# Four dense steps between the first two score blocks, a second buffer for a head's values, and later flips of the last normalised rows

## The chip, the cores and the metric

The kernel runs on one core of one Trainium2 chip. The metric is the device time of one execution in microseconds (us); the time of a kernel is the median of its runs. A core has a matrix engine (PE, TensorE), a vector engine (DVE), an activation engine (ACT), a general engine (POOL, GpSimd) and a queue engine that mostly issues DMAs (SP). Each works through its own instructions in order, and semaphores make one wait for another. PE reads its operands from on-chip memory (SBUF) and writes to an accumulation memory (PSUM), out of which DVE and ACT take the results. PE runs at 1.2 or 2.4 GHz; the profile gives the granted clock as a share of the full speed.

## The reference, cut to what matters

One layer of a streaming encoder is computed for a prompt of 1024 frames and for 8 decode streams of 16 frames. One input projection feeds two groups of heads: four heads of differential softmax attention and four heads of retention. Then come the output projection and a gated MLP with a causal convolution.

```python
h = rmsnorm(x, g_mix) * (1.0 + sc_m) + sh_m
qa, ka, va, qr, kr, vr, gr = split_projection(h, w_in, pos)
oa = attend(qa, ka, va)
orr, ret_state = retain(qr, kr, vr)
oa = rmsnorm(oa, g_sub_a) * (1.0 - lam_init)
...
def diff_attention_block(q, k, v, q_pos, k_pos, rel_bias, lam):
    ...
    def probs(qi, ki):
        s = jnp.einsum('bqhd,bkhd->bhqk', qi, ki).astype(jnp.float32) * scale + bias
        return jax.nn.softmax(jnp.where(visible, s, NEG_INF), axis=-1)
    p = (probs(q[..., :A_QK_DIM], k[..., :A_QK_DIM])
         - lam * probs(q[..., A_QK_DIM:], k[..., A_QK_DIM:]))
    return jnp.einsum('bhqk,bkhd->bqhd', p.astype(v.dtype), v)
```

For the prompt there are 8 query blocks of 128 rows in each of 4 heads. Block qb sees (qb + 1) * 128 keys, so the work of a block grows from 128 to 1024 columns. Each block needs two softmaxes, one for each half of the query and key vectors.

## The kernel before

The span falls into stages: norms and the conditioning vectors with the first projections (to about 238 us), prompt attention (238 to 460), decode attention (460 to 560), retention (560 to 650), output projection, up-projection and down-projection. The change touches the prompt attention alone.

**Two kinds of work on PE.** The attention loop (L695) runs over n_ = 8 * head + block. For each block it computes the scores of the next block (`scores`, L617: matmuls at L626 into two PSUM tiles `sc`, one for each softmax), flips the weights of the current block with PE transposes (`flip`, L649), and multiplies the flipped weights with the values (`weighted`, L661). Between these three, `fill(ns)` puts in dense steps. A dense step is one pass of the input projection for another head or another stage, three matmuls (L62, L63, L64) on the same accumulator `dn`. In the text a D is one such step. The numbers in `f_scores`, `f_flip` and `f_out` say for how many nanoseconds, by the program's own account, dense steps are put in; a 384-column D counts 480, a 256-column one 320. A step is taken only as long as the unit of work it belongs to lies below the limit `prog["lim"]`. The units are, in order, the k and q projections of heads 0 to 3 (two units for each head, 24 D's of 384 columns each), then 256-column units for retention. While head 0 runs, the limit is 4, so the stock is the 48 D's of head 1's k and q.

**What one block asks of the other engines.** After the scores, DVE adds the bias (L629), takes the row maximum (L631), and ACT takes the exponential into `e` and sums it (L632), once for each softmax. DVE then makes the reciprocal (L634), the factor (L635) and the difference of the two softmaxes, `e` in L637. Only then can PE flip `e` (F, L649); ACT copies the flipped tiles out of PSUM (`pT`, L651), and PE multiplies (W, L661). DVE scales the result (L662). The two `sc` tiles exist once for a block's two halves (bufs=2), so scores of the next block need the exponentials of this block to be done.

**Normalised rows.** After blocks 3 and 7 of a head, `small_norm` (L264 to L268, with L131 on DVE and L132 on POOL) normalises four blocks' rows, and `later(5000, ...)` queues `heads_out`: four transposes (H, L670), an ACT copy (L672) and a DMA to `d_m` (L673). A queued function runs in the first `step` or `fill` in which the program's own count of nanoseconds has passed its due time.

**Values and weights.** `load_v` (L611) loads a head's values, 512 KB, into `vt`; before, there is one buffer, so the load of the next head's values waits for the last W of this head. Weights come as `raw` tiles of 256 KB by DMA (L142), are cast by ACT (L58), and the remainder is taken by DVE (L59). Inside the attention loop, PE's order is the order in which the program is written; DVE, ACT, POOL and SP are put in order by a scheduler that works from its own estimates.

**Decode and retention.** After the loop, decode loads `qbd` (L718), `kc` (L728) and others on SP, behind the last `d_m` store, flips the cached keys (L744, copied by ACT at L746 and by DVE) and runs its scores. The 256-column D's left over are used there and in retention, where t = 8 multiplies with the decode streams' states (L1018), updates them (L1025 and L1028), stores them, and loads the next ones (L1047); the prompt blocks follow (L983, L985, L994).

Of the kernel before, what the change touches and what calls it, by code (L numbers as in the profile page):

```python
# [7 lines left out]
F32 = mybir.dt.float32  # L8
# [40 lines left out]
def body(ctx: ExitStack, tc: tile.TileContext, i):  # L49
# [4 lines left out]
    def pool(name, bufs=1, **kw):  # L54
        return tc.tile_pool(name=name, bufs=bufs, **kw)
# [65 lines left out]
    def tp():  # L121
        return psd.tile([128, 4, 128], F32, tag="tp", bufs=2, name="tp")
# [55 lines left out]
    units, pend, prog = [], [], {"cur": None, "bal": 0.0, "now": 0.0, "done": 0, "lim": 99, "rope": None}  # L178
# [4 lines left out]
    def can():  # L183
        return units and prog["done"] + (prog["cur"] is not None) < prog["lim"]
# [5 lines left out]
    def later(ns, fn):  # L190
        pend.append((prog["now"] + ns, fn))
# [17 lines left out]
    def fill(ns):  # L209
        prog["bal"] += ns  # L210
        while prog["bal"] > 0 and (can() or prog["cur"]):
            step()
        if prog["bal"] > 0:
            prog["now"] += prog["bal"]
            prog["bal"] = 0.0
        while pend and pend[0][0] <= prog["now"]:
            pend.pop(0)[1]()
# [317 lines left out]
    with ExitStack() as st:  # L535
        ap = st.enter_context(pool("attn"))
# [3 lines left out]
        def sc():  # L540
            return pva.tile([128, 1024], F32, tag="sc", bufs=2, name="sc")
# [67 lines left out]
            units.append([lambda: load_wt(base, h * 128), lambda w_: dense_t(nm, h, w_), None])  # L609

        def load_v(h):  # L611
            vt = ap.tile([128, 8, 128], F32, tag="vt", bufs=1, name="vt")
            nc.sync.dma_start(vt, i["v_prompt"][:, h * 128:h * 128 + 128].rearrange("(t p) d -> p t d", p=128))
            return vt

        def scores(h, kq, qb):
            khi, klo, qs = (kq[z_] for z_ in ("khi", "klo", "qs"))  # L617
            nk = (qb + 1) * 128
            e = ap.tile([128, 2, SEQ], F32, tag="e", bufs=2, name="e")
            sm = ap.tile([128, 8], F32, tag="sm", bufs=3, name="sm")  # L620
            for hf in range(2):
                s_ = sc()
                for c in range(0, nk, 512):
                    n = min(512, nk - c)
                    for p, kk in enumerate((khi, klo)):
                        T.matmul(s_[:, c:c + n], lhsT=qs[:, hf, qb * 128:qb * 128 + 128],  # L626
                                 rhs=kk[:, hf, c:c + n], start=(p == 0), stop=(p == 1))
                lo_ = max(nk - 256, 0)
                V.tensor_tensor(out=s_[:, lo_:nk], in0=s_[:, lo_:nk],  # L629
                                in1=nb[:, h, 256 - (nk - lo_):256], op=ALU.add)  # L630
                V.tensor_reduce(out=sm[:, hf:hf + 1], in_=s_[:, 0:nk], op=ALU.max, axis=AX.X, negate=True)  # L631
                S.activation(out=e[:, hf, 0:nk], in_=s_[:, 0:nk], func=ACTF.Exp,  # L632
                             bias=sm[:, hf:hf + 1], scale=1.0, accum_out=sm[:, 2 + hf:3 + hf])
            V.reciprocal(out=sm[:, 4:6], in_=sm[:, 2:4])  # L634
            V.scalar_tensor_tensor(out=sm[:, 6:7], in0=sm[:, 2:3], scalar=sm[:, 5:6], in1=nlam,  # L635
                                   op0=ALU.mult, op1=ALU.mult)
            V.scalar_tensor_tensor(out=e[:, 0, 0:nk], in0=e[:, 1, 0:nk], scalar=sm[:, 6:7],  # L637
                                   in1=e[:, 0, 0:nk], op0=ALU.mult, op1=ALU.add)
            return e, sm
# [15 lines left out]
        def weighted(h, vt, qb, e, sm, pTs):  # L655
            if qb % 4 == 0:
                o4s[0] = ap.tile([128, 4, 128], F32, tag="o4", bufs=2, name="o4")
            o4 = o4s[0]
            po = tp()[:, 0]
            for n in range(qb + 1):  # L660
                T.matmul(po[:, 0:128], lhsT=pTs[n // 4][:, n % 4], rhs=vt[:, n], start=(n == 0), stop=(n == qb))  # L661
            V.tensor_scalar_mul(o4[:, qb % 4], po[:, 0:128], sm[:, 4:5])  # L662
            if qb % 4 == 3:
                small_norm(ap, o4, 4)
                later(5000, lambda: heads_out(h, qb, o4))

        def heads_out(h, qb, o4):
            p_ = tp()
            for n in range(4):
                T.transpose(p_[:, n], o4[:, n], ident)  # L670
            om = ap.tile([128, 512], F32, tag="t2", bufs=2, name="om")
            S.activation(out=om, in_=p_.rearrange("p a b -> p (a b)"), func=ACTF.Copy, scale=g_sa)  # L672
            nc.sync.dma_start(d_m[h, :, qb // 4 * 512:qb // 4 * 512 + 512], om)  # L673
# [5 lines left out]
        def spare():  # L679
# [4 lines left out]
        build_nb()  # L684
        drain(2)
        vt = load_v(0)
        cur = (0, vt, 0) + scores(0, kqs[0], 0)
        f_scores = ([1500, 1250, 1150, 1200, 650, 850, 450, 650],
                    [1950, 1850, 1750, 1650, 1550, 1450, 1350, 1250])
        f_flip = ([1925, 1775, 1625, 1475, 1325, 1325, 1475, 1025],  # L690
# [3 lines left out]
        for n_ in range(8 * NH):  # L694
            h, qb = divmod(n_, 8)  # L695
            nxt = None
            if n_ < 8 * NH - 1:
                h2, qb2 = divmod(n_ + 1, 8)
                if qb2 == 0:
                    drain(2 * h2 + 2)  # L700
                    vt = load_v(h2)
# [953 lines left out]
```

## Time and profile before

| what | value |
|---|---|
| time before, median of 3 runs | 1548.28 us (1547.75 to 1548.39) |
| time of the profiled execution | 1546.16 us |
| span of the profiled execution | 1544.3 us |
| PE busy | 1502.5 us, 97% |
| DVE busy | 964.3 us, 62% |
| ACT busy | 601.4 us, 39% |
| POOL busy | 232.2 us, 15% |

The span runs from the first to the last instruction of the profiled execution; 1.86 us of its time lie around the span. Busy time is an average over stages with different limits. The rows that matter are those in which PE waits, since PE is busy almost throughout. In a row of the timeline the first number is the start and the second the duration; matmuls are pipelined, so the time that one costs is the distance between starts, and not its duration.

### The profile page before, as it was taken

To read this page: it belongs to the slowest core of one execution; us is meant where nothing else is said; L and a number is where in the kernel's file an instruction comes from. 1 tells how busy PE (TensorE), PEld (TensorE's weight loads), DVE (VectorE), ACT (ScalarE), POOL (GpSimd) and SP (SyncE) were. 2 spreads that over 40 slices of the span, in tenths; PEclk is the share of its full clock that TensorE was granted. 3 is DMA by queue.
4 is the path that set the end of the run, shared out by engine and by line. 5 is a ranking of instruction groups with operands and counts; after the bars stand their busy time and mean duration, and the time that the engine had idled before them with its cause. 6 is when DMAs were issued, how large, how long until landed. Compare 5 with 4: busy or idle time off the path is not lost.

```text
span 1544.3 us, 27022 instructions
## 1 busy us (share of the span) xinstructions
PE 1502.5 (97%) x10580; PEld 1369.4 (89%) x10580; DVE 964.3 (62%) x1735; ACT 601.4 (39%) x1167; POOL 232.2 (15%) x335
## 2 busy tenths in 40 slices
PE   6999999999999999999999999999999999999998
PEld 5867899999898898878899999999999988888786
DVE  4701237888765424553499877877788758254695
ACT  4501124555332433455564444444444455021212
POOL 1000021111121111343212111110111100000051
PEclk8999999999999999999999999999999999999999
DMA  9865331111319657675532222222222237132232
GB/s 295 270 253 181 121 107 49 54 46 50 110 61 338 217 200 222 224 249 191 171 119 86 82 73 74 72 71 80 77 75 71 80 119 270 35 116 88 95 134 109
DMA packets 191515, 205.98 MB, mean 133 GB/s; under 512 B 11357, under 2 KB 149899, under 8 KB 191388
## 3 DMA queue, kind: packets, MB, share of 16 engines
q1 hardware_dynamic: 172412, 189.31, 37.7%
q10 hardware_dynamic: 18976, 14.95, 3.0%
q8 instruction: 83, 1.36, 0.4%
q14 instruction: 44, 0.36, 0.1%
HBM read 154.66 MB, written 49.56 MB: 132 GB/s over the span
## 4 chain that ended last, share of the span: by engine, by line
PE 56%; DVE 2%; DMA 1%; issue 0%; ACT 0%; SPq 0%; POOL 0%; POOLq 0%; DVEq 0%; ACTq 0%
PE pb L1342 5%; PE pb L1344 5%; PE pb L1343 5%; PE dn L62 3%; PE dn L64 3%; PE dn L63 3%; PE pf L64 3%; PE pf L63 3%; PE pf L62 3%; PE dn L1342 2%; PE dn L1344 2%; PE dn L1343 2%; PE tp L1342 2%; PE tp L1344 2%; PE tp L1343 2%; PE tp L63 2%
## 5 line engine op out<-in xcount | busy, mean ns | idle before, releaser
L62 PE MATMUL dn<-w,hhi 128*128 128x256 f32 x648 | 189.7, 293 | 0.0
L64 PE MATMUL dn<-w,hlo 128*128 128x256 f32 x648 | 181.9, 281 | 0.0
L63 PE MATMUL dn<-w,hhi 128*128 128x256 f32 x648 | 181.6, 280 | 0.0
L62 PEld LDWEIGHTS dn<-w,hhi 128*128 128x128 f32 x648 | 122.5, 189 | 11.4 <-issue 10.2
L64 PEld LDWEIGHTS dn<-w,hlo 128*128 128x128 f32 x648 | 122.6, 189 | 7.5 <-issue 7.5
L63 PEld LDWEIGHTS dn<-w,hhi 128*128 128x128 f32 x648 | 122.7, 189 | 4.3 <-issue 4.2
L1288 DVE SCALAR_TENSOR_TENSOR y<-U,cv,y 128x1168 f32<-128x1168 f32 x88 | 124.2, 1429 | 3.0 <-ACT y L1285 2.1
L58 ACT CAST sl<-raw 128x512 fp32r<-128x512 f32 x65 | 40.3, 622 | 108.8 <-PE pb L1343 93.7
L58 ACT CAST se<-raw 128x512 fp32r<-128x512 f32 x66 | 41.1, 624 | 100.2 <-PE dn L1343 48.4
L62 PE MATMUL dn<-hhi,w 128*128 128x384 f32 x192 | 69.9, 364 | 0.0
L246 POOL TENSOR_TENSOR sg<-sg,rot 128x256 f32<-128x256 f32 x36 | 28.1, 780 | 272.2 <-DVE rot L245 229.5
L63 PE MATMUL dn<-hlo,w 128*128 128x384 f32 x192 | 65.0, 339 | 0.0
L64 PE MATMUL dn<-hhi,w 128*128 128x384 f32 x192 | 65.0, 339 | 0.0
L1294 POOL COPY tails<-U 128x18 f32<-128x18 f32 x44 | 23.7, 538 | 271.7 <-DVE U L1359 183.1
L59 DVE TENSOR_TENSOR w<-raw,w 128x512 fp32r<-128x512 f32 x56 | 39.0, 712 | 37.0 <-ACT w L58 24.7
L1285 ACT ACTIVATE y<-U,cv 128x1168 f32<-128x1168 f32 x44 | 60.2, 1367 | 4.5 <-DVE U L1363 0.5
L1514 DVE TENSOR_TENSOR facc<-facc,pf 128x512 f32<-128x512 f32 x54 | 36.8, 681 | 39.0 <-PE pf L64 39.0
L632 ACT ACTIVATE e<-sc,sm 128x128 f32<-128x128 f32 (+7 forms) x64 | 47.3, 744 | 30.9 <-DVE sm L631 30.1
L62 PE MATMUL dn<-woh,mh 128*128 128x512 f32 x144 | 57.9, 402 | 0.0
L58 ACT CAST w<-raw 128x512 fp32r<-128x512 f32 x56 | 33.3, 619 | 60.3 <-PE dn L63 33.8
L58 ACT CAST ew<-wr 128x512 fp32r<-128x512 f32 x24 | 14.6, 619 | 108.1 <-PE tp L63 84.2
L64 PE MATMUL dn<-woh,ml 128*128 128x512 f32 x144 | 56.5, 393 | 0.0
(427 smaller groups left out, 4861.8 us busy)
## 6 DMA issues: line engine op xcount, KB each, us to landing
wa<-in_w_ada SPq DMA_DIRECT2D x48, 512.0 KB, 8.6
raw<-in_w_up SPq DMA_DIRECT2D x88, 256.0 KB, 2.9
raw<-in_w_in SPq DMA_DIRECT2D x56, 256.0 KB, 4.2
wr<-in_w_down SPq DMA_DIRECT2D x48, 256.0 KB, 3.7
gr<-d_g SPq DMA_DIRECT2D x20, 576.0 KB, 3.7
d_g<-y SPq DMA_DIRECT2D x22, 512.0 KB, 2.6
kc<-in_cache_k SPq DMA_DIRECT2D x8, 1024.0 KB, 7.9
vc<-in_cache_v SPq DMA_DIRECT2D x8, 1024.0 KB
```

What stands on the lines that cost most here:

```text
L58: S.copy(hi, src)
L59: V.tensor_tensor(out=lo, in0=src, in1=hi.bitcast(F32), op=ALU.subtract)
L62: T.matmul(out, lhsT=sh, rhs=mh, start=first, stop=False)
L63: T.matmul(out, lhsT=sh, rhs=ml, start=False, stop=False)
L64: T.matmul(out, lhsT=sl, rhs=mh, start=False, stop=last)
L632: S.activation(out=e[:, hf, 0:nk], in_=s_[:, 0:nk], func=ACTF.Exp, bias=sm[:, hf:hf + 1], scale=1.0, accum_out=sm[:, 2 + hf:3 + hf])
L1285: S.activation(out=y[:, j0:j1], in_=U[:, j0:j1], func=ACTF.Identity, scale=wconv[0][:, kt:kt + 1], bias=bconv[:, kt:kt + 1])
L1288: V.scalar_tensor_tensor(out=y[:, j0:j1], in0=U[:, j0 + j:j1 + j], scalar=wconv[j][:, kt:kt + 1], in1=y[:, j0:j1], op0=ALU.mult, op1=ALU.add)
L1342: T.matmul(o, lhsT=sh, rhs=mh, start=st_, stop=False, skip_group_check=True)
L1343: T.matmul(o, lhsT=sh, rhs=ml, start=False, stop=False, skip_group_check=True)
L1344: T.matmul(o, lhsT=sl_, rhs=mh, start=False, stop=en, skip_group_check=True)
L1514: V.tensor_tensor(out=facc[t][:, sl], in0=facc[t][:, sl], in1=p_, op=ALU.add)
```

## The change

There are three edits, all in the prompt attention. The tile `vt` gets two buffers. `heads_out` of block 7 is queued with 8000 instead of 5000. And behind the scores of the very first block, before the loop, `fill(1920)` with the limit 4 puts in four D's.

```diff
         def load_v(h):
-            vt = ap.tile([128, 8, 128], F32, tag="vt", bufs=1, name="vt")
+            vt = ap.tile([128, 8, 128], F32, tag="vt", bufs=2, name="vt")
...
-                later(5000, lambda: heads_out(h, qb, o4))
+                later(8000 if qb == 7 else 5000, lambda: heads_out(h, qb, o4))
...
         cur = (0, vt, 0) + scores(0, kqs[0], 0)
+        prog["lim"] = 4
+        fill(1920)
```

The number of D's and of every other PE instruction is the same; only their places differ. PE, at the start of the loop, between the scores of block 0 (128 columns) and those of block 1 (256 columns) of head 0:

```order
 L626 MATMUL sc<-khi,qs 128x128
 L626 MATMUL sc<-klo,qs 128x128
+L62 MATMUL dn<-hhi,w 128x384
+L63 MATMUL dn<-hlo,w 128x384
+L64 MATMUL dn<-hhi,w 128x384
...
 L626 MATMUL sc<-khi,qs 128x256
 L626 MATMUL sc<-klo,qs 128x256
```

Four D's now stand there. Since head 0 has a fixed stock of 48, its end has four fewer: of four D's between the last-but-one flip and its W three are left, and the three D's behind that W are gone, so that PE goes from this W straight to the scores of head 1's block 0, the last flip and the last W of head 0.

DVE at the same place, the end of head 0, before; `e` with 1024 columns is the last block of head 0, `sc` with 128 columns the first block of head 1, `qs` and `w` belong to dense work:

```order
L631 TENSOR_REDUCE sm<-sc 128x1
L585 SCALAR_TENSOR_TENSOR qs<-dn,qs 64x384
L631 TENSOR_REDUCE sm<-sc 128x1
L634 RECIPROCAL sm<-sm 128x2
L635 SCALAR_TENSOR_TENSOR sm<-sm,nlam 128x1
L662 TENSOR_SCALAR o_2836<-tp,sm 128x128
L637 SCALAR_TENSOR_TENSOR e<-e,sm 128x1024
L629 TENSOR_TENSOR sc<-sc,nb 128x128 x2
L59 TENSOR_TENSOR w<-raw,w 128x512
L631 TENSOR_REDUCE sm<-sc 128x1 x2
```

And DVE there in the changed kernel:

```order
L631 TENSOR_REDUCE sm<-sc 128x1
L59 TENSOR_TENSOR w<-raw,w 128x512
L662 TENSOR_SCALAR o_2848<-tp,sm 128x128
L629 TENSOR_TENSOR sc<-sc,nb 128x128
L634 RECIPROCAL sm<-sm 128x2
L631 TENSOR_REDUCE sm<-sc 128x1
L585 SCALAR_TENSOR_TENSOR qs<-dn,qs 64x256
L635 SCALAR_TENSOR_TENSOR sm<-sm,nlam 128x1
L629 TENSOR_TENSOR sc<-sc,nb 128x128
L59 TENSOR_TENSOR w<-raw,w 128x512
L637 SCALAR_TENSOR_TENSOR e<-e,sm 128x1024
```

Between the last row maximum of head 0 and L637 there now stand two L59, both bias adds and one row maximum of head 1 and one L585; the L585 between the two row maxima is gone from there. At block 4 of head 0, an L585, a bias add and L266 have likewise moved in front of L637.

The flips H behind block 7 move on PE as follows. In heads 0 to 2, H comes some blocks' work later in the next head; in head 3's start, the H of head 2 stood right before the scores of block 2 and now stands behind them and behind the flip of block 1. The last H, at the end of the attention, has 25 D's of 256 columns ahead of it and behind the last W, where it had 16; 29 D's follow before decode's first PE instruction (L814) as before. The 9 D's come out of retention: 26 instead of 31 stand before the last group of L1018, and the 5 before L983 are gone.

ACT at the start of decode, before, from the copy of the last H:

```order
L672 ACTIVATE om<-tp,cv 128x512
L253 DMA d_qr<-sg 128x256
L58 CAST w<-raw 128x512 x3
L253 DMA d_qr<-sg 128x256 x2
L746 COPY KT<-tp 128x512
L58 CAST w<-raw 128x512
L746 COPY KT<-tp 128x512
```

And in the changed kernel, where line numbers behind the third edit are higher by two:

```order
L672 ACTIVATE om<-tp,cv 128x512
L58 CAST w<-raw 128x512
L253 DMA d_qr<-sg 128x256
L58 CAST w<-raw 128x512 x2
...
L58 CAST w<-raw 128x512
L253 DMA d_qr<-sg 128x256
L748 COPY KT<-tp 128x512 x2
```

Six casts stand ahead of the first copy of flipped keys, where three stood.

On SP, `vt` of heads 0 and 1 are issued together before the loop; those of heads 2 and 3 are issued earlier, and the eighth `raw` of the weights that are loaded at the start of head 3 no longer stands behind `vt`. In retention, four `raw` loads of the output projection's weights (L1082) and `mraw` and `sgr` now stand ahead of the first store of `d_on` (L1041), and the stores of the states and the loads of the next ones come as 3 stores, 1 load, 1 store, 3 loads instead of 2, 1, 2, 3. On DVE in retention, one more L59 of the output projection's weights stands ahead of the state updates L1028. On ACT, the eighth cast of head 3's weights now stands ahead of the copy `pT` of head 3's block 0 (L651).

## Rows read from the trace of the kernel before

**Rows 1.** Part 1 of the page: busy time, share of the span and number of instructions of each engine.

```profile
PE 1502.5 (97%) x10580; PEld 1369.4 (89%) x10580; DVE 964.3 (62%) x1735; ACT 601.4 (39%) x1167; POOL 232.2 (15%) x335
```

**Rows 2.** Windows: stretch and its length, busy time of each engine with its instructions, granted clock of PE, share of the DMA engines' time, GB/s.

```profile
400.00:405.00 5.00, 4.65 (x25) 4.68 (x26) 3.78 (x11) 1.30 (x2) 0.72 (x1) 0.66 0.42 144
...
475.00:480.00 5.00, 4.45 (x41) 3.32 (x40) 4.01 (x9) 2.45 (x6) 2.08 (x3) 1.00 1.05 386
480.00:560.00 80.00, 79.98 (x944) 71.44 (x944) 36.16 (x91) 30.13 (x57) 8.30 (x14) 1.00 0.64 217
...
600.00:602.00 2.00, 2.00 (x34) 1.53 (x30) 0.00 (x0) 0.57 (x5) 0.00 (x0) 0.50 0.00 0
...
620.00:625.00 5.00, 3.84 (x35) 3.60 (x34) 2.86 (x8) 2.10 (x10) 2.23 (x3) 1.00 0.99 336
```

**Rows 3.** Waits of PE from 225 to 520 us: tile and line that waited, what released it, the sum, the number of times, the longest.

```profile
PE sc L626 <- ACT e L632: 1.7, 1, 1.7
...
PE tp L661 <- DMA vt<-out_v_prompt: 0.8, 2, 0.5
PE tp L649 <- DVE e L637: 0.5, 2, 0.2
```

**Rows 4.** Timeline of PE at the start of the loop: the last score matmul of block 0, the scores of block 1, the first D, the first flip. In brackets the idle time before and what ended it.

```profile
238.53 0.27 PE L626 MATMUL sc<-klo,qs 128*128 128x128 f32 x1
240.48 0.39 PE L626 MATMUL sc<-khi,qs 128*128 128x256 f32 x1 [1.67 <-ACT e L632]
...
241.42 0.52 PE L62 MATMUL dn<-hhi,w 128*128 128x384 f32 x1
241.74 0.52 PE L63 MATMUL dn<-hlo,w 128*128 128x384 f32 x1
...
244.77 0.27 PE L649 MATMUL tp<-ident_all,e 128*128 128x128 f32 x1
```

**Rows 5.** Timeline of DVE there: the difference of the two softmaxes of block 0.

```profile
242.97 0.35 DVE L637 SCALAR_TENSOR_TENSOR e<-e,sm 128x128 f32<-128x128 f32 x1
```

**Rows 6.** Timeline of PE at the end of head 0: the last D, the scores of head 1's block 0, the last flip and the last W of head 0.

```profile
286.25 0.34 PE L62 MATMUL dn<-hhi,w 128*128 128x384 f32 x1
...
286.77 0.23 PE L626 MATMUL sc<-khi,qs 128*128 128x128 f32 x1
...
287.30 1.06 PE L649 MATMUL tp<-ident_all,e 128*128 128x128 f32 x8
288.73 1.49 PE L661 MATMUL tp<-vt,pT 128*128 128x128 f32 x11 [0.37 <-ACT pT L651]
```

**Rows 7.** Timeline of DVE there.

```profile
282.19 0.56 DVE L585 SCALAR_TENSOR_TENSOR qs<-dn,qs 64x384 fp32r<-64x384 f32 x1
...
285.28 0.17 DVE L634 RECIPROCAL sm<-sm 128x2 f32<-128x2 f32 x1 [1.27 <-ACT e L632]
...
285.88 1.28 DVE L637 SCALAR_TENSOR_TENSOR e<-e,sm 128x1024 f32<-128x1024 f32 x1
287.15 0.52 DVE L629 TENSOR_TENSOR sc<-sc,nb 128x128 f32<-128x128 f32 x2
287.57 0.68 DVE L59 TENSOR_TENSOR w<-raw,w 128x512 fp32r<-128x512 f32 x1
288.17 0.48 DVE L631 TENSOR_REDUCE sm<-sc 128x1 f32<-128x128 f32 x2
...
289.29 0.42 DVE L585 SCALAR_TENSOR_TENSOR qs<-dn,qs 64x256 fp32r<-64x256 f32 x1
```

**Rows 8.** Timelines of SP, ACT, DVE and PE at the start of head 3: the last `raw` load behind `vt`, its cast, the L59 behind the cast, and the flip H of head 2's last rows.

```profile
392.52 0.37 SPq L142 DMA_DIRECT2D raw<-in_w_in  x1
...
397.88 0.62 ACT L58 CAST w<-raw 128x512 fp32r<-128x512 f32 x1 [2.94 <-DMA raw<-in_w_in]
...
398.53 0.69 DVE L59 TENSOR_TENSOR w<-raw,w 128x512 fp32r<-128x512 f32 x1 [1.99 <-ACT w L58]
...
400.35 0.63 PE L670 MATMUL tp<-ident_all,o 128*128 128x128 f32 x4 [1.92 <-DVE sm L635]
```

**Rows 9.** Timelines of PE, SP and ACT at the start of decode: the last H, the first decode instruction, the first flip of cached keys; the first `kc` load; the first copy of flipped keys and the fourth cast.

```profile
459.04 0.60 PE L670 MATMUL tp<-ident_all,o 128*128 128x128 f32 x4
...
469.55 0.51 PE L814 MATMUL tp<-hk,ident_all 64*128 64x144 f32 x2
471.50 0.66 PE L744 MATMUL tp<-ident_all,kc 128*128 128x128 f32 x4 [1.45 <-DMA kc<-in_cache_k]
...
464.13 0.45 SPq L728 DMA_DIRECT2D kc<-in_cache_k  x1
...
472.99 0.59 ACT L746 COPY KT<-tp 128x512 f32<-128x512 f32 x1 [8.03 <-PE tp L744]
474.42 0.62 ACT L58 CAST w<-raw 128x512 fp32r<-128x512 f32 x1 [0.84 <-DMA raw<-in_w_in]
```

**Rows 10.** Timelines of PE, DVE and SP in retention: the last group of L1018, the last wait of L994; the state updates that DVE runs ahead of L985; the first load of the output projection's weights.

```profile
599.48 1.92 PE L1018 MATMUL rt<-sb,Qd 128*32 128x128 f32 x26 [1.39 <-DMA sb<-in_state_ret]
...
622.97 0.49 PE L994 MATMUL rt<-ld,AT 128*128 128x128 f32 x2 [1.16 <-DVE AT L985]
...
604.50 1.66 DVE L1028 SCALAR_TENSOR_TENSOR sb<-sb,rt 128x128 f32<-128x128 f32 x8
...
611.26 0.40 SPq L1082 DMA_DIRECT2D raw<-in_w_out  x1
```

## The prediction

> **What bounds the kernel now.** I read the page first: PE is busy for 1502.5 us, 97% of the span, and no other engine comes near [rows 1]. So an edit that moves PE instructions without changing their number is worth only what it does to PE's idle time and to its clock. The list of PE's waits in the attention comes next. The reader is to see that they are few: 1.7 us for the scores of block 1, 0.8 us in two waits for values, 0.5 us for the difference of the softmaxes [rows 3]. Then I went to each place that the diff touches, in the timeline, and asked what PE waits for there. The windows give the clock: after some waits PE runs for a stretch at 1.2 instead of 2.4 GHz (0.66 as the mean from 400 to 405 us, 0.50 from 600 to 602), and after others not (1.00 from 475 to 480, behind a wait of 1.45 us) [rows 2, 9].
>
> **The front of the loop.** Before, PE waits 1.67 us for the exponentials of block 0, since both `sc` tiles are taken. Then comes a stretch at half clock: matmuls of a D start 0.32 us apart [rows 4], where the last D of head 0 has three in 286.25 to 286.77, 0.52 us, 0.173 each [rows 6]. The four D's that are put in take 4 x 0.52 = 2.08 us, more than the 1.67 us, so the wait goes, and with it the slow stretch, if that follows from the wait. From the scores of block 1 to the first flip it is 244.77 - 240.48 = 4.29 us for scores of four matmuls of 256 columns and four D's; at the full rate the D's are 2.08, and the scores 0.46 (a D of 256 columns, three matmuls, takes 0.35 below), so 1.75 us are lost. What is late next is the first flip: it needs L637, which ends at 242.97 + 0.35 = 243.32 [rows 5]. With four D's, the scores and the four D's that follow, PE arrives at 238.81 (1.67 before 240.48) + 2.08 + 0.46 + 2.08 = 243.4, so there is no new wait. Gain 1.67 + 1.75 = 3.4 us; from 1.7 (the clock stays low anyway) to 3.4.
>
> **The end of head 0.** The four D's are taken from a stock and are missing behind the flip of block 6. Their cover is gone: before, L637 ends at 285.88 + 1.28 = 287.16, and the last flip starts at 287.30, behind the scores of head 1 [rows 6, 7]. The slack is 0.14 us, so 2.08 us of D's become 2.08 us of wait. Second, DVE's order: before L637 there now stand, beyond what stood there, two L59, two bias adds, a row maximum and an L585. DVE waits 1.27 us for the exponential before L634 [rows 7]; the first L59 and the first bias add fit in there. What follows L634 is a row maximum, an L585, a bias add and an L59: by starts about 0.24 + 0.4 + 0.2 + 0.6 = 1.5 us, and the L585 between the row maxima (0.56 us) is gone, so L637 comes 1.0 us later. Bounds: -0.56 (all of it hides) and +1.5. Third, the clock: the new wait, 2.08 + 1.0 - 0.14 = 2.9 us, is longer than the 1.67 us behind which the clock fell [rows 4], so I count a slow stretch, at 1.5 us somewhat below the losses of 1.75 here and 1.7 in head 3 (0 to 1.75). Fourth, at block 4 an L585, a bias add and L266 have moved ahead of L637. Nothing shows this wait; the nearest rows are an operation of 0.56 us, three of which would make 1.6 [rows 7], and the flips' waits for L637, of at most 0.2 us [rows 3]. I take 0.5, nearer to the waits that exist, of 0 to 1.6. Together 2.1 + 1.0 + 1.5 + 0.5 = +5.1 us, from +1.5 (2.08 - 0.56) to +6.9.
>
> The Trainium skill, page "TensorE: Matmul & The Clock Gate", section "Part 1: The HAM clock gate", says that the array's clock follows an activity window that runs on freely and doesn't start anew with the work. By that rule the same pause can be followed by a slow stretch in one place and not in another, which agrees with the waits of 1.67 and 1.45 us above. By the rows alone the term is 1.5 us; by the rule, without it, the sum below would be 1.5 us lower.
>
> **Two buffers for the values.** They take away the waits for `vt`, 0.8 us in two, the longer of them 0.5 [rows 3]. The first goes. The second is at head 3's block 0, where the copy `pT` now stands behind a cast that waits for the eighth `raw` (below), so I count 0.5 of the 0.8, of 0.3 to 0.8. Two loads side by side before the loop hold up nothing that shows.
>
> **The flip of block 7.** In heads 0 and 1 it waited for nothing, and later placement costs nothing. Head 2's H waits 1.92 us: L268 stood behind an L59, this behind a cast, and the cast behind the DMA that was issued at 392.52 and landed by 397.88 [rows 8]. Behind it the clock is low: 0.66 over 5 us means (1 - 0.66)/0.5 x 5 = 3.4 us at half clock, or 1.7 us lost [rows 2]. Now the scores of block 2 and more D's come ahead of H, and it is ready by then: gain 3.6. Against it, the cast stands ahead of `pT` of block 0; if the `raw`, no longer behind `vt`, lands about 1.2 us sooner, W(3,0) still waits some 0.4 us. So -3.2, from -3.6 to 0 (the DMA lands as late as before and W takes over the wait).
>
> **The last H.** Nine D's more stand ahead of it. A D of 256 columns takes (469.55 - 459.4)/29 = 0.35 us: 29 stand between H, whose four transposes from 459.04 take some 0.36, and L814 [rows 9]. H, the store of `d_m` and every load behind it on SP, `qbd` and `kc` among them, come 9 x 0.35 = 3.15 us later. Decode is PE-bound from 480 to 560 (79.98 of 80 us) [rows 2], so it cannot catch up; what could is retention, from which the D's are taken. There they stood ahead of L1018, which waits 1.39 us for states, and ahead of L983, after which L994 waits for DVE's L1028 [rows 10]. With fewer D's these waits grow by as much, so nothing comes back. One L59 more ahead of L1028 delays the stores and with them the states: +0.7, as L59 lasts [rows 7]. But the weight loads of the output projection move ahead, from 611 us into a stretch without transfers (600 to 602: 0 GB/s), out of one in which the DMA engines are full (0.99) [rows 2, 10]; the late wait of L994, 1.16 us, should go. Sum 3.15 + 0.7 - 1.16 = +2.7, from 0 (retention gives the D's back) to +3.9.
>
> **Sum.** -3.4 + 5.1 - 0.5 - 3.2 + 2.7 = +0.7 us. The profiled execution took 1546.16 us, 1.86 of them outside its span of 1544.3; it becomes 1546.9. It lies 2.1 us under the median of the runs, so for the median I add the same difference: 1548.28 + 0.7 = 1549.0 us. Two gains and two losses of about equal size are the whole of it. I call a difference within 0.2%, 3.1 us, no change: it is about what a measurement of this kernel can tell.
>
> **Rivals.**
> - *The end of head 0 is cheap.* DVE's added operations fall into its wait of 1.27 us, and the clock stays up: +1.5 instead of +5.1, so the sum is -2.9, 1545.4 us. For it speaks that the wait of 1.45 us cost no clock; against it that DVE's row maximum and L59 stand behind L634, not ahead of it.
> - *Retention gives the D's back.* If the states are there when L1018 comes, the last H costs -0.5 instead of +2.7: the sum is -2.5, 1545.8 us. Against it speak the waits on both sides of these D's. With the first rival together: -6.1, 1542.2 us, clearly faster.
> - *Slower: the start of decode on ACT.* The first copies of flipped keys now stand behind six casts. Before, the fourth of these ran at 474.42, after a wait for its `raw`, and the first copy at 472.99 [rows 9]. If the copies have to wait for that cast and two more (0.62 each), the first comes at about 474.42 + 3 x 0.62 = 476.3, 3.3 us later, PE's flips run out of tiles, and the sum is +4.0, 1552.3 us. It decides once the sixth `raw` lands later than L744's first tile is full. Against it: the casts are earlier in the queue, and the loads may come sooner beside a later `kc`.
> - *The change doesn't do what it says* at head 3: the `raw` lands no sooner, and `pT`, now behind its cast, hands W the wait that H had. Then the -3.2 is 0, the sum +3.9, 1552.2 us.
>
> **Chances.** My forecast as worked out 0.32 (no change 0.27, slower 0.05); a cheap end of head 0 alone 0.18 (half of it faster); retention alone 0.14 (half faster); both 0.11 (faster); decode's casts 0.18 (nearly all slower, 0.16); head 3 0.07 (slower 0.06). Faster: 0.09 + 0.07 + 0.11 = 0.27. Slower: 0.05 + 0.16 + 0.06 = 0.27. No change: 0.46. The range reaches from the middle between the two cheap cases and their sum, 1543.5, to 1554, where the decode rival meets a term at its upper bound. The forecast's own range is 1546.5 to 1551.5.
>
> **What would show it.** In the profile of the changed kernel: no wait for L632 before the scores of block 1, and 1.00 as the clock behind it; a wait of 2 to 4 us for L637 before the last flip of head 0, with a clock below 1 behind it; no wait for `vt`; no wait before head 2's H; the last H, counted from the last W, 3.1 us later, and longer waits at L1018. I am wrong on the whole if the wait at the end of head 0 is under 1 us, if L744 or L756 wait over 3 us at decode's start, or if the time between the last H and the end of retention shrinks by more than 3 us.

## The result, and the profile after

The changed kernel takes 1558.76 us (median of 4 runs, 1557.69 to 1561.0), the kernel before 1548.34 us beside it. The ratio is 1.0073, with a 95% interval of 1.0058 to 1.0089: 10.4 us slower. The forecast was 1549.0 us and no change, with a range to 1554; the measured time lies outside it.

The profiled execution took 1561.0 us, the longest of the four, with a span of 1559.2 against 1544.3. Part of this has nothing to do with the change: the first score matmul of the attention starts at 242.44 instead of 238.25, although the instructions of PE, DVE, ACT and POOL up to there are the same in the same order. Over the profiled executions below whose earlier stages keep this order, it starts between 237.4 and 242.4; the 237.4 belongs to a kernel (experiment 6) whose loads up to there are those of the changed kernel too. So the table gives each place as its distance from the first score matmul. It is made from the first or last start that the trace gives for a line.

| us from the first score matmul to | before | after | difference |
|---|---|---|---|
| last W of the attention (L661) | 215.0 | 214.6 | -0.4 |
| last H (L670) | 221.1 | 223.9 | +2.8 |
| decode's first instruction (L814, after: L816) | 231.3 | 241.8 | +10.5 |
| decode's first score matmul (L756, L758) | 236.9 | 247.2 | +10.2 |
| decode's last score matmul | 307.0 | 317.2 | +10.2 |
| last L994 (L996) of retention | 405.4 | 415.9 | +10.5 |
| first up-projection (L1342, L1344) | 547.3 | 557.9 | +10.6 |
| end of the span | 1306.1 | 1316.8 | +10.7 |

The whole loss lies in one place, between the last W and decode's first instruction: 3.2 us more to the last H, and 7.8 us more from there on. The attention loop, in which all three edits stand, came out 0.4 us shorter, and from decode's first score matmul to the end only half a microsecond is added.

The waits of PE in the changed kernel, from 240 to 500 us (tile, line, releaser, sum, times, longest), answer to [rows 3]:

```profile
PE tp L649 <- DVE e L637: 4.9, 4, 2.9
PE dn L62 <- DVE rot L245: 4.1, 1, 4.1
PE dn L63 <- DVE w L59: 0.8, 2, 0.7
PE tp L661 <- ACT pT L651: 0.6, 2, 0.4
PE dn L62 <- ACT w L58: 0.5, 1, 0.5
PE sc L626 <- ACT e L632: 0.3, 1, 0.3
```

The waits that the change was said to remove are gone: the 1.67 us for L632, those for `vt`, that before head 2's H. The flips' waits for L637 have grown from 0.5 to 4.9 us. And there are three kinds of wait that stood in no row before: dense steps that wait for the rotary work of DVE (`rot`, L245) and for weights from ACT (L58) and DVE (L59).

**The front**, timeline of PE, beside [rows 4]:

```profile
242.73 0.28 PE L626 MATMUL sc<-klo,qs 128*128 128x128 f32 x1
242.84 0.39 PE L62 MATMUL dn<-hhi,w 128*128 128x384 f32 x1
...
244.97 0.29 PE L626 MATMUL sc<-khi,qs 128*128 128x256 f32 x1
...
247.59 0.33 PE L649 MATMUL tp<-ident_all,e 128*128 128x128 f32 x1
```

No wait stands between the two score blocks, and the four D's behind them run at the full rate. From the last score matmul of block 0 to the first flip it is 4.86 us; before, it was 6.24 with four D's fewer.

**The end of head 0**, timelines of PE and of DVE, beside [rows 6, 7]:

```profile
289.83 0.30 PE L626 MATMUL sc<-khi,qs 128*128 128x128 f32 x1 [0.30 <-ACT e L632]
...
293.13 1.94 PE L649 MATMUL tp<-ident_all,e 128*128 128x128 f32 x8 [2.88 <-DVE e L637]
294.94 3.36 PE L661 MATMUL tp<-vt,pT 128*128 128x128 f32 x14
...
289.87 0.15 DVE L634 RECIPROCAL sm<-sm 128x2 f32<-128x2 f32 x1
289.99 0.29 DVE L631 TENSOR_REDUCE sm<-sc 128x1 f32<-128x128 f32 x1
290.31 0.42 DVE L585 SCALAR_TENSOR_TENSOR qs<-dn,qs 64x256 fp32r<-64x256 f32 x1
290.76 0.22 DVE L635 SCALAR_TENSOR_TENSOR sm<-sm,nlam 128x1 f32<-128x1 f32 x1
290.90 0.29 DVE L629 TENSOR_TENSOR sc<-sc,nb 128x128 f32<-128x128 f32 x1
291.10 0.68 DVE L59 TENSOR_TENSOR w<-raw,w 128x512 fp32r<-128x512 f32 x1
291.70 1.28 DVE L637 SCALAR_TENSOR_TENSOR e<-e,sm 128x1024 f32<-128x1024 f32 x1
```

PE waits 2.88 us for L637, behind four operations that used to come after it. Eight flips then take 1.94 us where they took 1.06: the clock is low.

**The start of decode**, timelines of PE, DVE, ACT and SP, beside [rows 9]:

```profile
466.02 0.60 PE L670 MATMUL tp<-ident_all,o 128*128 128x128 f32 x4
...
470.18 0.35 PE L62 MATMUL dn<-w,hhi 128*128 128x256 f32 x1 [0.48 <-ACT w L58]
...
481.44 0.55 PE L62 MATMUL dn<-w,hhi 128*128 128x256 f32 x1 [4.09 <-DVE rot L245]
...
484.27 0.84 PE L816 MATMUL tp<-hk,ident_all 64*128 64x144 f32 x2
...
480.47 0.42 DVE L242 TENSOR_TENSOR sg<-dn,rope 128x256 f32<-128x256 f32 x1 [8.18 <-DMA rope<-in_rope]
...
469.46 1.14 ACT L58 CAST w<-raw 128x512 fp32r<-128x512 f32 x2 [0.58 <-DMA d_m<-om]
...
471.10 0.45 SPq L730 DMA_DIRECT2D kc<-in_cache_k  x1
471.59 0.50 SPq L812 DMA_DIRECT2D rope<-in_rope  x1
```

PE stands still for 4.09 us in the middle of the dense steps, since DVE waits 8.18 us for the `rope` tile. That tile is loaded on SP behind the store of `d_m`, which follows H, and behind `qbd` and the first `kc`. Two casts of weights wait for the same store of `d_m`, and with them PE waits 0.48 us for weights. The windows (stretch, busy times, granted clock, DMA share, GB/s) show what follows, at the end of head 0 and here:

```profile
293.00:298.00 5.00, 4.87 (x22) 4.64 (x23) 1.34 (x5) 2.17 (x6) 0.31 (x1) 0.50 0.23 74
...
481.00:487.00 6.00, 5.56 (x23) 5.09 (x24) 4.45 (x10) 1.86 (x3) 1.87 (x2) 0.50 1.06 383
```

Behind both waits PE runs for 5 to 6 us at 1.2 GHz. Half of PE's busy time in such a stretch is lost: about 2.8 us at the start of decode. At the end of head 0 the next 2 us still have 0.69, so that it is about 3 us there.

**Why the tile is needed just then.** The dense unit whose blocks end in the rotary step has two sources of its angles. The unit that runs out behind the last H loads a small `cs` tile for each block. The next one, taken up in decode, uses `rope`. 29 D's stand between H and decode's first instruction in both kernels. Before, 18 of them finish the old unit and 11 belong to the new one; now the old unit has got 9 of its D's ahead of H, so 9 and 20. A block takes 8 D's, and there are two `dn` accumulators. So 16 D's of the new unit can run without `rope`, and the 17th needs DVE to have emptied a block; the D that waits 4.09 us above, at 481.44, is the 17th. A row of the kernel before shows the same tile arriving, then without harm to PE:

```profile
473.69 0.42 DVE L242 TENSOR_TENSOR sg<-dn,rope 128x256 f32<-128x256 f32 x1 [0.80 <-DMA rope<-in_rope]
474.23 0.28 DVE L245 TENSOR_TENSOR rot<-dn,rope 128x128 f32<-128x128 f32 x1
...
476.60 0.39 PE L62 MATMUL dn<-w,hhi 128*128 128x256 f32 x1
```

The row of PE is the 17th D, and DVE had finished with the block at 474.5, 2.1 us earlier. DVE's first use of `rope` starts 473.69 - 459.04 = 14.65 us after H before, and 480.47 - 466.02 = 14.45 us after it now: the tile follows H at nearly the same distance.

### The profile page after: what moved, and what is told of

Same layout as the page of the kernel before. It is cut to its first block, busy times and chain, and to the rows that moved or that the text cites. A ratio compares the mean times of both kernels' runs of the same rounds, so it can differ in the third digit from the quotient of the medians.

```text
span 1559.2 us, 27024 instructions
## 1 busy us (share of the span) xinstructions
PE 1511.0 (97%) x10580; PEld 1375.9 (88%) x10580; DVE 964.2 (62%) x1735; ACT 603.2 (39%) x1169; POOL 231.2 (15%) x335
## 4 chain that ended last, share of the span: by engine, by line
PE 54%; DVE 3%; DMA 1%; ACT 1%; issue 1%; POOL 0%; SPq 0%; POOLq 0%; DVEq 0%; ACTq 0%
PE pb L1344 5%; PE pb L1345 5%; PE pb L1346 5%; PE dn L64 3%; PE dn L62 3%; PE dn L63 3%; PE pf L64 3%; PE pf L62 3%; PE pf L63 3%; PE dn L1344 2%; PE dn L1346 2%; PE dn L1345 2%; PE tp L1344 2%; PE tp L1346 2%; PE tp L1345 2%; PE tp L63 2%
## 5 line engine op out<-in xcount | busy, mean ns | idle before, releaser
L58 ACT CAST sl<-raw 128x512 fp32r<-128x512 f32 x65 | 40.3, 622 | 107.4 <-PE pb L1345 95.7
L58 ACT CAST se<-raw 128x512 fp32r<-128x512 f32 x66 | 41.0, 623 | 100.5 <-PE dn L1345 48.4
L632 ACT ACTIVATE e<-sc,sm 128x128 f32<-128x128 f32 (+7 forms) x64 | 47.4, 745 | 39.8 <-DVE sm L631 39.5
L59 DVE TENSOR_TENSOR w<-raw,w 128x512 fp32r<-128x512 f32 x56 | 38.7, 708 | 37.5 <-ACT w L58 25.1
L58 ACT CAST w<-raw 128x512 fp32r<-128x512 f32 x56 | 33.6, 620 | 67.4 <-DMA raw<-in_w_in 30.9
L58 ACT CAST ew<-wr 128x512 fp32r<-128x512 f32 x24 | 14.5, 619 | 109.9 <-PE tp L63 85.8
```

The costliest lines, as they stand in the source:

```text
L58: S.copy(hi, src)
L59: V.tensor_tensor(out=lo, in0=src, in1=hi.bitcast(F32), op=ALU.subtract)
```

## The experiments

Theory A says that the later last H is the loss, by way of what is loaded behind it; A1 names the `rope` tile as the larger part. Theory B puts the loss on head 0's end, theory C on the second buffer for the values.

**1. All edits but the last H.**

```diff
-                later(8000 if qb == 7 else 5000, lambda: heads_out(h, qb, o4))
+                later(8000 if qb == 7 and h < 3 else 5000, lambda: heads_out(h, qb, o4))
```

> All three edits, but the last flip H of the attention (head 3, block 7) keeps its 5000. Theory A (the start of decode: the later H makes the loads behind it late, and nine D's more of the unit that needs the rope tile stand before decode's first instruction): the whole loss of 10.4 us goes; the attention loop alone came out 0.4 us shorter in the profiled execution, so 1548 us, and no wait for rot L245. Theory B (the missing D's at the end of head 0 and DVE's order there are the loss): it stays, 1555 us or more. Theory C (the second buffer for the values changes the order on SP and ACT, and the start of decode suffers from that): it stays too, 1555 us or more, with the waits at decode's start.

Measured: 1549.27 us beside 1546.0 for the kernel before on that chip, ratio 1.0021 (1.0005 to 1.0038). The waits for rot L245 and for weights are gone; the loop is 0.4 us shorter than before, and so is the way to decode's first score matmul. The waits of PE from 240 to 500 us:

```profile
PE tp L649 <- DVE e L637: 4.9, 4, 2.9
PE tp L746 <- DMA kc<-in_cache_k: 2.0, 2, 1.5
PE tp L661 <- ACT pT L651: 0.7, 2, 0.4
PE sc L626 <- ACT e L632: 0.3, 1, 0.3
```

Theories B and C fall as the main cause. With the last H goes most of the loss: 6.6 us by the traces (the span from the first scores is 4.1 us longer than before instead of 10.7), 8 us by the ratios. The 3 to 4 us that remain are not in the attention: the profiled execution, the slowest of the ten and 4.3 us above their median, loses 2.1 us between decode's first scores and the end of retention and another 1.8 up to the up-projection. The 2.1 us are longer waits of PE in retention: 7.7 us instead of 5.6, of which 3.3 instead of 2.1 for the states and a new one of 1.1 for ACT's `sg`. The 1.8 us stand behind a wait of 1.73 us for DVE's `xn`, where the granted clock is 0.66 over 5 us; in the kernel before, behind its wait of 1.52 us there, it is 1.00. What makes the waits in retention longer stays open.

**2. The later flips alone** (the line of the changed kernel, in the kernel before).

> The later flips of block 7 alone, in all heads; one buffer for the values and no D's between the first two score blocks. Theory A: +10.9 us at the start of decode and about -3.2 us at head 3's start, 1556 us, with the wait of 4 us for rot L245. Theory B: faster than before by the 3 us of head 3, 1545 us. Theory C: the same as B, since the values have one buffer.

Measured: 1554.46 us beside 1546.0, ratio 1.0047 (1.0024 to 1.0069). The loop is 3.8 us shorter, and from the last W to decode's first score matmul it is 9.9 us longer, with a wait of 4.43 us for rot L245. That is theory A: this edit alone makes both the gain at head 3 and the loss at decode.

**3. The four D's at the front alone** (the last two lines of the change).

> The four D's between the first two score blocks alone. Theory A: in the trace of the changed kernel head 0 cost 3.4 us net of a gain of 0.3 at the values' wait, so +3.7 us, 1552 us. Theory B: most of the 10.4 us, 1556 us or more. Theory C: no wait at decode's start, so as A.

Measured: 1547.58 us beside 1546.0, ratio 1.0016 (1.0004 to 1.0028). The loop is 4.2 us longer, where 3.7 was expected; of this, the medians show 1.6 us and the ratio 2.5. Either way the edit is a loss, and a small part of the whole.

**4. Two buffers for the values, and the later flips in heads 0 to 2 only.**

> Two buffers for the values and the later flips of block 7 in heads 0 to 2 only: no D's at the front, the last H as before. Theory A: the 0.8 us of the values' waits and about 3.4 us at head 3's start are gained and nothing is lost, 1544 us, faster than before. Theory B: the same, 1544 us. Theory C: the start of decode is slow, 1554 us or more.

Measured: 1542.87 us beside 1546.0, ratio 0.998 (0.9969 to 0.999). The loop is 4.1 us shorter. Faster than both kernels, and theory C falls a second time. But 1.3 of the 4.1 us are no work of the edits. At the front, where PE has the order and the wait of the kernel before, the clock did not fall; the windows start at the end of the wait, in the kernel before and here:

```profile
240.40:245.40 5.00, 4.92 (x20) 4.84 (x21) 4.09 (x13) 2.58 (x11) 0.00 (x0) 0.66 0.45 131
...
242.15 0.39 PE L626 MATMUL sc<-khi,qs 128*128 128x256 f32 x1 [1.67 <-ACT e L632]
...
242.10:247.10 5.00, 4.95 (x28) 4.61 (x29) 4.07 (x13) 2.44 (x10) 0.00 (x0) 1.00 0.44 131
```

The first flip comes 1.4 us sooner here without any edit at that place. At head 3 the edits give 3.6 us, and a new wait of 1.3 us in head 1, of the flips of projected keys (L558) for DVE's L662, takes part of it back.

**5. The rope tile loaded early, in the changed kernel.**

```diff
+        rope0 = aux.tile([128, NT, 2, 64], F32, tag="rope0", bufs=1, name="rope")
+        nc.sync.dma_start(rope0, i["rope"].rearrange("(t p) a d -> p t a d", p=128))
         vt = load_v(0)
...
-        prog["rope"] = dp.tile([128, NT, 2, 64], F32, name="rope")
-        nc.sync.dma_start(prog["rope"], i["rope"].rearrange("(t p) a d -> p t a d", p=128))
+        prog["rope"] = rope0
```

> The changed kernel with all three edits; only the rope tile (576 KB) is a tile of its own, loaded before the attention loop instead of at the start of decode, so that DVE's first use of it waits for nothing; the last H stays at 8000. Theory A1 (the rope tile is the larger part: both accumulators are full and PE can't begin the 17th D of the unit that needs it): no wait for rot L245, decode's first instruction comes about 6 us sooner than in the changed kernel (4.1 of wait and 1.9 of low clock), and the time is 1553 us where the changed kernel takes 1558.8. Theory A2 (the late d_m and the weights' casts behind it hold PE): the wait moves to the casts, and the time stays at 1557 us or more.

Measured: 1559.58 us beside 1545.85, ratio 1.0088 (1.0068 to 1.0107): the time did not fall. The trace shows why. The wait for rot L245 is gone, and decode's first score matmul comes 6.9 us sooner after the first scores, as A1 says. Two things take it back. The first scores start at 244.9 us, 2.4 us later than in the changed kernel: the scheduler issued the load early in the first stage, ahead of loads of the conditioning weights, and reordered DVE and ACT there. And of the 6.9 us, 3.1 are lost again between decode's first score matmul and the end. So this run alone does not settle A1. The experiment was repeated in 9 with the order of the first stage kept.

**6 and 7. The last H at 6500 and at 6900**, in the changed kernel.

> The changed kernel with the last H at 6500 instead of 8000 (8000 in heads 0 to 2): 21 D's ahead of it instead of 25, 28 behind. By the count of D's, 15 of the unit that needs the rope tile then stand before decode's first instruction, one fewer than two full accumulators. Theory A1: no wait for rot L245; from the first scores to decode's first score matmul it is 1.5 us longer than before (5 D's of 0.35 less 0.5 of the loop), and the time is 1550 us. Rival, a price for each D that H comes later (11 us over 9 D's): 5.5 us longer, 1554 us.

> The same with 6900: 22 D's ahead of H, 29 behind, so 17 of that unit before decode's first instruction, one more than two full accumulators. Theory A1: the wait for rot L245 is there, 4 us or more, with a low clock behind it; 7 us longer than before up to decode's first score matmul, 1555 us. Rival with a price for each D: 6.5 us longer, 1554.5 us, so this run tells little alone, and much beside the one with 6500.

Measured: 1555.33 us with 6500 and 1555.27 us with 6900, ratio 1.0057 in both (1.0039 to 1.0076 and 1.0041 to 1.0073). For 6500 the expectation of A1 failed. There is no wait before decode's first instruction, which comes 0.4 us later after the first scores than before. But behind it:

```profile
471.16 0.66 PE L746 MATMUL tp<-ident_all,kc 128*128 128x128 f32 x4 [1.61 <-DMA kc<-in_cache_k]
471.57 0.37 PE L62 MATMUL dn<-w,hhi 128*128 128x256 f32 x1
474.30 0.55 PE L62 MATMUL dn<-w,hhi 128*128 128x256 f32 x1 [2.13 <-DVE rot L245]
```

The D at 471.57 is the 16th of the new unit and the one at 474.30 the 17th. So the count of two accumulators is right, but I had read it as a threshold at decode's first instruction. What decides is when PE comes to the 17th D, wherever that stands, against the arrival of `rope`. Each D that H is put behind moves `rope` 0.35 us later and the 17th D sooner, so the cost grows with every D. With 6900 the 17th D comes before decode's first instruction and waits 2.96 us, where 4 or more was expected. From the last W to decode's first score matmul it is 5.5 us longer with 5 D's more, 7.6 with 6 and 10.6 with 9, or 1.1 to 1.3 for each D, near the rival's price of 1.2. Counted from the first scores, as the expectations are, it is 4.4 us longer with 6500, between A1's 1.5 and the rival's 5.5, and 5.8 with 6900.

**8. The front's four D's taken from another place**, on the kernel of experiment 4.

```diff
         cur = (0, vt, 0) + scores(0, kqs[0], 0)
+        prog["lim"] = 4
+        fill(1920)
...
-            fill(f_flip[h // 3][qb])
+            fill(f_flip[h // 3][qb] - (960 if n_ < 2 else 0))
```

> Two buffers for the values, the later flips in heads 0 to 2, the last H as before, and the four D's between the first two score blocks, but taken from between flip and W of blocks 0 and 1 of head 0 (two each) instead of from its end. Theory D (the four D's at the front are worth 3.4 us, and what takes it back is their absence and DVE's order at head 0's end): the loop is 4.2 + 3.4 = 7.6 us shorter than before, no wait of over 0.5 us at the last flip of head 0, and the time is 3 us below the same kernel without the front, 1540 us beside 1543. Rival E (DVE paces head 0, so D's taken out anywhere in it come back as waits for L637): no shorter than without the front, 1543 us, with waits at the flips of blocks 2 to 7.

Measured: 1541.45 us beside 1545.85, ratio 0.9974 (0.9961 to 0.9987). The loop is 6.4 us shorter than before, where 7.6 was expected, and 2.3 more than in experiment 4. The expectation had added the front's 3.4 us to the 4.2 of experiment 4, which had the better clock at the front in it already. Head 0 now ends as it did before the change:

```profile
283.61 1.06 PE L649 MATMUL tp<-ident_all,e 128*128 128x128 f32 x8
285.04 2.05 PE L661 MATMUL tp<-vt,pT 128*128 128x128 f32 x16 [0.37 <-ACT pT L651]
```

Theory D holds, with a smaller gain: the D's at the front are worth 2.3 us beside a kernel whose clock stayed up there, and the place from which they were taken was the loss. DVE does not pace the whole of head 0. By the runs this kernel is the fastest one tried; against experiment 4 the difference, 0.9974 to 0.998, lies within the intervals, and only the trace shows it.

**9. The rope tile of its own, its load held back**, in the changed kernel; the tile's pool is opened ahead of the attention.

```diff
+    rp_st = ExitStack()
+    rope0 = rp_st.enter_context(pool("ro")).tile([128, NT, 2, 64], F32, name="rope")
...
+            if n_ == 15:
+                G.tensor_copy(rope0[:, 0, 0, 0:1], nxt[4][:, 6:7])
+                nc.sync.dma_start(rope0, i["rope"].rearrange("(t p) a d -> p t a d", p=128))
...
-        prog["rope"] = dp.tile([128, NT, 2, 64], F32, name="rope")
-        nc.sync.dma_start(prog["rope"], i["rope"].rearrange("(t p) a d -> p t a d", p=128))
+        prog["rope"] = rope0
```

> As the run with an early rope tile, with the load held back: a one-column copy on GpSimd from a softmax sum of head 2's first block into the rope tile makes its DMA wait until head 2, so that the stages before the attention keep their order on every engine. Theory A1: as there, no wait for rot L245 and decode's first score matmul 6.9 us sooner after the first scores than in the changed kernel, and now the time follows: 1552 us, 7 below the changed kernel. If the time stays at 1558 us although the trace shows the stage shorter, then the stages behind give it back, and A1 names a wait that was not the loss.

Measured: 1551.92 us beside 1545.64, ratio 1.0041 (1.0027 to 1.0055), where the changed kernel has 1.0073. Waits of PE from 240 to 500 us; line numbers of the attention are higher by two:

```profile
PE tp L651 <- DVE e L639: 4.7, 4, 2.9
PE tp L663 <- ACT pT L653: 1.6, 3, 0.7
PE dn L63 <- DVE w L59: 0.8, 2, 0.7
PE dn L62 <- ACT w L58: 0.5, 1, 0.5
PE sc L628 <- ACT e L634: 0.3, 1, 0.3
```

The wait of 4.09 us is gone and nothing has taken its place; the waits for weights are still there. This is the run that settles A1: of the 10.2 us at decode's first score matmul 6.0 go, and the time goes with them, by 5 us in the ratios. From the last W to decode's first score matmul it is still 5.5 us longer than before: nine D's at 0.35, the waits for weights of 1.3 us in all, and a stretch at 1.2 GHz behind these, less the wait of 1.45 us for `kc` that is gone.

**10 and 11. The same on the kernel of experiment 8, and there with the last H at 4400.**

> The kernel with two buffers for the values, later flips in heads 0 to 2 and the four D's at the front taken from blocks 0 and 1 of head 0 (1541.5 us), with the rope load held back in the same way. Theory A1 says nothing of a gain at rot L245 here, since there is no such wait; but 576 KB fewer beside the first kc load should shorten PE's wait of 2.5 us for kc by 1.5 us (576 KB at 380 GB/s): 1540 us. If kc is bound by its own issue and not by the bytes beside it: 1541.5 us.

> The same, with the last H at 4400 instead of 5000: 14 D's ahead of it instead of 16. The loads behind it start 0.7 us sooner. If the wait for kc is what is left at decode's start, another 0.7 us go, 1539.5 us; if H then waits for its normalised rows (ready 0.8 us before it now), the two cancel and the time is that of the run beside it.

Measured: 1542.45 us beside 1545.64, ratio 0.9978 (0.9959 to 0.9997), and 1543.89 us, ratio 0.999 (0.9974 to 1.0006). The wait for `kc` is 2.32 us without the rope load beside it, where it was 2.53: in these two executions the bytes of `rope` are no more than 0.2 us of it. The times of the two can't be set against each other for that, since behind the wait of 2.32 us the clock is 0.70 over 5.7 us, and behind the one of 2.53 us it stayed at 1.00. With H earlier the wait is 1.09 us, and decode's first score matmul comes 2.6 us sooner; but by the end of retention the kernel is 1.4 us behind the one beside it. There the waits for the states are about the same, 2.6 us instead of 2.4, but behind the first of them the clock is 0.50 over 6.7 us, which is 3 us lost, where experiment 10 has 1.00. Neither is an improvement.

## Why the prediction was wrong

Point by point, by its own steps:

- *The front*: forecast -3.4 us. Measured: first flip 1.38 us sooner with four D's (2.08 us) more done, 3.46 us. Right beside this execution of the kernel before. But 1.4 us of it are the clock, and experiment 4 had the same wait of 1.67 us and kept a clock of 1.00. That the kernel before lost them in this execution is luck; the lower bound of 1.7 is the gain without them, though it was argued otherwise, by a clock that stays low.
- *The end of head 0*: forecast +5.1, with a wait of 2.9 us at the last flip. The wait is 2.88 us: missing D's and DVE's order were sized right. The low clock lasted longer than the row at the front had shown: it lost about 3 us and not 1.5, and the bound was 1.75. The wait at block 4's flip is 1.39 us, where I took 0.5 from 0 to 1.6. The last W of head 0 comes 3.6 us later after the first scores than before, so the end and block 4 cost 3.6 + 3.5 = 7.1 us, just above the upper bound of 6.9.
- *The values and head 2's H*: forecast -0.5 and -3.2. From the last W of head 2 to the last W of head 3 the changed kernel is 3.6 us shorter. Right. In it no wait of PE is left at `vt`, and H has none.
- *The last H*: forecast +2.7, from 0 to +3.9. Measured from the last W to decode's first score matmul: +10.6. This is the step that failed; of the 10 us by which the sum is off, 8.4 lie behind the last W and 1.6 in the loop. The 3.2 us by which H came later and the finding that retention gives nothing back were right. What the step said of the loads was that they "come 9 x 0.35 = 3.15 us later", and it went on as if a later load only moved the work behind it. It named `qbd` and `kc`, for which decode waits, and left out the `rope` tile, for which the dense steps ahead of decode wait. So it never asked how many of the 29 D's behind H need something that is loaded behind H. Their number went from 11 to 20.

The 10.6 us come out of the rows as follows. H is 3.2 us later. Between H and L816 PE waits 0.48 + 0.67 + 0.17 us for weights, whose casts are held until `d_m` is stored, and 4.09 us for rot L245, together 5.4. The low clock behind it, 0.50 over 6 us, takes 2.8 us. The wait of 1.45 us for `kc` is gone, since `kc` has landed meanwhile. That is 3.2 + 5.4 + 2.8 - 1.45 = 9.95; the rest of 0.7 is not accounted for.

That retention gives nothing back shows in its waits of PE, two lines of the kernel before and two of the changed one:

```profile
PE rt L994 <- DVE AT L985: 3.5, 3, 1.5
PE rt L1018 <- DMA sb<-in_state_ret: 2.1, 2, 1.4
...
PE rt L1020 <- DMA sb<-in_state_ret: 3.7, 4, 1.5
PE rt L996 <- DVE AT L987: 1.1, 2, 0.8
```

The waits for the states grew, as the prediction's signs said, and the wait of 1.16 us for L985 went. What takes up the rest is the clock: 0.50 over 10.2 us around the longer waits, where it was 0.50 over 3.3 us before.

The rival that saw the right place, decode's start, had the wrong engine: the copies of flipped keys on ACT behind six casts, +4.0 us. The casts waited, but no wait of PE for a copy `KT` shows at decode's start. The rival of a cheap end of head 0 is refuted by the 2.88 us, that of retention by the constant difference in the table.

The Trainium skill, page "TensorE: Matmul & The Clock Gate", section "Part 1: The HAM clock gate", was used for the doubt whether a wait costs clock, since its activity window runs on freely. The runs agree with it, though they don't show such a window: behind a wait for `kc` of 2.61 us (experiment 4) the clock is 0.73 over the next 6 us, behind one of 2.53 us (experiment 8) it is 1.00.

## What to carry to other kernels

When a step is put off, list what is queued behind it on every queue, and then ask of the work that runs between the step and the old point of need which of it uses something from that list; it is this work, and not the stage for which the load is named, that stops first. Filler work that is taken from a stock has a price at the place from which it is taken: the four D's paid 3.5 us at the front and cost 7.1 at block 4 and the end of head 0, together with DVE's new order there; taken from two blocks with slack, they left 3.2 of the 3.5 us at the end of block 3. A load that waits for nothing may be moved by a scheduler to a place where it harms others, so a test that frees a load must also hold it where it is meant to be. And before a gain or a loss of 1 to 3 us in one profiled execution is put down to an edit, the granted clock behind each wait has to be set beside that of another execution with the same wait.

## What was not expected of the hardware

The stages ahead of the attention, with the same instructions of the four computing engines in the same order, took between 237.4 and 242.4 us in the profiled executions; two kernels that differ by 3 us can't be told apart by one execution each, but their stages can, counted from a common instruction.

The stretch at 1.2 GHz behind a wait is not of one length, not even behind the same wait at the same place. Behind the wait of 1.67 us at the front the clock was 0.66 over the next 5 us in the kernel before and in experiment 2, and 1.00 in experiment 4. Behind the wait of 2.88 us at the end of head 0 it was 0.55 to 0.57 over the next 7 us in the changed kernel and in experiments 1, 3 and 5, and 0.76 in experiments 6, 7 and 9; here the changed kernel and experiment 6:

```profile
293.10:300.10 7.00, 6.97 (x33) 6.73 (x34) 2.51 (x8) 2.17 (x6) 0.31 (x1) 0.56 0.19 60
...
288.10:295.10 7.00, 6.25 (x36) 6.01 (x37) 2.77 (x10) 2.08 (x6) 0.31 (x1) 0.76 0.17 56
```

That is 3.1 us lost in the one and 1.7 in the other. And the distance from the last H to DVE's first use of the `rope` tile was 14.4 to 15.0 us in seven of the nine executions whose kernels load it behind H, and 15.6 and 15.7 in experiments 8 and 4.
